# LRU gates of a recurrent block computed by tanh of half their argument

## The chip, the cores and the metric

One core of a Trainium2 chip. The metric is the device time of one execution in microseconds (us); runs of the kernel before and of the changed one are compared. TensorE is called PE, VectorE DVE, ScalarE ACT, GpSimd POOL, SyncE SP.

## What is computed

The program is a small encoder in fp32, of a recurrent block with its feed-forward part and an attention block with its own; the model width is 1024, the sequence 16 meta tokens and 512 others. The change touches the gated linear recurrence (LRU) of the recurrent block, 1536 channels wide:

```python
def rg_lru(x, w_r, b_r, w_i, b_i, lam):
    xb = x.reshape(bsz, length, N_LRU_BLOCKS, LRU_BLOCK)
    r = jax.nn.sigmoid(jnp.einsum('blnc,ncd->blnd', xb, w_r).reshape(bsz, length, width) + b_r)
    i = jax.nn.sigmoid(jnp.einsum('blnc,ncd->blnd', xb, w_i).reshape(bsz, length, width) + b_i)
    log_a = -LRU_C * r.astype(jnp.float32) * jax.nn.softplus(-lam.astype(jnp.float32))
    a = jnp.exp(log_a)
    u = jnp.sqrt(-jnp.expm1(2.0 * log_a)) * (i * x).astype(jnp.float32)
    ...
    _, h = lax.associative_scan(combine, (a, u), axis=1)
    return h.astype(x.dtype)

def recurrent_mixer(x, w_in, conv_w, conv_b, w_r, b_r, w_i, b_i, lam, w_out):
    ...
    rec = causal_dwconv(rec, conv_w, conv_b)
    h = rg_lru(rec, w_r, b_r, w_i, b_i, lam)
    return (jax.nn.gelu(gate) * h) @ w_out
```

There are 16 blocks of 96 channels, and `LRU_C` is 8.

## The kernel before, in words

Channels lie on the 128 partitions and tokens along the free axis, 528 of them, worked on in two halves of 272 and 256. The 1536 recurrent channels are 12 chunks of 128, and three chunks are one group of the LRU. Every number is kept as a high part, rounded to the multiplier's format, and a low part; a product is three matmuls (`project`, L188). Weights come by DMA, 512 KB at a time, into three buffers; ACT casts the high part (L162), and DVE or POOL subtracts for the low part (through the helper `tt`, L118). The helpers `tt` (L118), `stt` (scalar_tensor_tensor, L121) and `act` (L124) record most operations, so in the trace these carry the helper's line.

The recurrent block is cut into steps, each with the number of a chunk or group:

- R, `recurrent_in` (L762): the projection of one chunk, 24 matmuls for each half into a PSUM bank; ACT evacuates the bank with scale and bias, DVE reads it three times more for the convolution's other taps (L775), and `split` (L216) makes high and low parts.
- S, `stack` (L724): eight DMAs on SP's queue gather rows of a group's chunks, so that blocks of 96 channels meet chunks of 128. The LRU step of that group multiplies the gathered rows.
- L, `lru` (L783): for each of three chunks, two gates and two halves, a group of five matmuls and an activation on ACT, twelve in all; then an exponential and a tanh for each chunk, then three square roots, and then on DVE the products and the scan (L823).
- G, `gate_project` (L829): the projection of a chunk of the output gate, evacuated by an ACT copy; E, `gate_gelu` (L853): its gelu; F, `gate_finish` (L858): the product with the LRU's result, and its split.

R and G take their banks in turn from the same four (`gbank(0, 4)`): R6's halves take two, G2's the other two, R7's halves the two of R6 again, each as soon as DVE has read it for the last time. L takes its banks from four others.

Before, ACT goes through three tables in an LRU step: sigmoid for the gates, then exponential and tanh, then square root. The compiler puts an ACT_TABLE_LOAD before each activation that needs another table than the one in place; the gelus of the G and E steps need one as well.

PE's order is written out by hand, as the string below (L39); the other engines' order is found by a scheduler when the kernel is built, from priorities (`tc.high_priority`) and from its own estimates of when work becomes ready. Only the LRU's activations and the gelus are tied to their order in the program (`order="lru"`).

```python
ORDER = "S0 G0 R3 R4 G1 R5 L0 S1 R6 G2 R7 L1 G3 R8 S2 G4 R9 E0 E1 E2 L2 F0 G5 F1 R10 F2 R11 S3 G6 L3 " \
    "E3 E4 E5 G7 F3 G8 F4 F5 G9 E6 E7 E8 F6 F7 F8 G10 E9 F9 G11 E10 F10 E11 F11"
```

Of the kernel before, what the change touches and what calls it, by code (L numbers as in the profile page):

```python
# [8 lines left out]
F32 = mybir.dt.float32  # L9
F32R = mybir.dt.float32r  # L10
AF = mybir.ActivationFunctionType
ALU = mybir.AluOpType
# [5 lines left out]
KD, KR, KF = D // 128, RNN // 128, FF // 128  # L18
# [22 lines left out]
P_ACW, P_ACB, P_BR, P_BI, P_LAM = 0, 48, 60, 72, 84  # L41
# [37 lines left out]
def trunk(ctx: ExitStack, tc: tile.TileContext, d, out):  # L79
    nc = tc.nc  # L80
    const = ctx.enter_context(tc.tile_pool(name="const", bufs=1))
# [13 lines left out]
    prm = const.tile([128, NPRM], F32, name="prm")  # L95
    cst = const.tile([128, 272], F32, name="cst")
    small = const.tile([128, 176], F32, name="small")
# [7 lines left out]
    def col(i):  # L105
        return prm[:, i:i + 1]
# [4 lines left out]
    def kept(x, engine):  # L111

        if line[0]:
            tc.stamp_issue_order_token(x.ins, line[0] + engine)
        return x

    def tt(eng, o, a, b, op):
        return kept(eng.tensor_tensor(o, a, b, op=op), "v" if eng is nc.vector else "p")  # L118

    def stt(o, a, s, b, op0, op1):  # L120
        return kept(nc.vector.scalar_tensor_tensor(o, in0=a, scalar=s, in1=b, op0=op0, op1=op1), "v")  # L121

    def act(o, i, f, order=None, **k):
        x = nc.scalar.activation(o, i, f, **k)  # L124
        if order:
            tc.stamp_issue_order_token(x.ins, order)
            return x
        return kept(x, "a")
# [53 lines left out]
    def mm(ps, w, x, first, last):  # L182
        nc.tensor.matmul(ps, lhsT=w, rhs=x, start=first, stop=last)  # L183
# [42 lines left out]
    def tok(a, n):  # L226
        return slice(PAD + a, PAD + a + n)

    A = slice(PAD, SLOT)
# [16 lines left out]
    def log1p_series(o, e, t1, t2):  # L246

        nc.vector.tensor_scalar(t1, e, 2.0, None, op0=ALU.add)
        nc.vector.reciprocal(t2, t1)
        tt(nc.vector, t1, e, t2, ALU.mult)  # L250
        tt(nc.vector, t2, t1, t1, ALU.mult)
        nc.vector.tensor_scalar(o, t2, 1.0 / 15.0, None, op0=ALU.mult)
        for n in (13, 11, 9, 7, 5, 3):
            stt(o, o, 1.0 / n, t2, ALU.add, ALU.mult)
        stt(o, o, 1.0, t1, ALU.add, ALU.mult)
        nc.vector.tensor_scalar(o, o, 2.0, None, op0=ALU.mult)

    m8, p4 = small[:, 0:12], small[:, 12:24]

    def decay_rates():  # L260
        lam = prm[:, P_LAM:P_LAM + KR]
        w0, w1, w2, w3 = (small[:, 40 + 12 * i:52 + 12 * i] for i in range(4))
        act(w0, lam, AF.Abs)
        act(w0, w0, AF.Exp, scale=-1.0)
        log1p_series(w3, w0, w1, w2)
        nc.vector.tensor_scalar(w1, lam, -1.0, 0.0, op0=ALU.mult, op1=ALU.max)
        tt(nc.vector, w1, w1, w3, ALU.add)
        nc.vector.tensor_scalar(m8, w1, -8.0, None, op0=ALU.mult)
        nc.vector.tensor_scalar(p4, w1, 4.0, None, op0=ALU.mult)
        nc.sync.dma_start(cst, d["cst"])  # L270
        nc.sync.dma_start(fb, d["fb"])

    for k in range(KD):
        w = x32[k // 2][k % 2].f[:, A]
        with tc.high_priority(EARLY):
            nc.sync.dma_start(w, d["x"][k])
        W_rec0.get(3 * k)
        with tc.high_priority(AHEAD):
            split(xs[k], w, A)
        if k == 1:  # L280
            nc.sync.dma_start(prm[:, :P_FC], d["prm"][:, :P_FC])
        if k == KD - 1:
            nc.sync.dma_start(prm[:, P_FC:], d["prm"][:, P_FC:])
            decay_rates()
# [431 lines left out]
    def gbank(first, n):  # L716
        used[first] = used.get(first, -1) + 1
        return fresh_bank(first + used[first] % n)
# [3 lines left out]
    xc, ax, stacks = [], [], {}  # L722
# [60 lines left out]
    def lru(g):  # L783
        gates = []
        for mc in range(3):
            m = 3 * g + mc
            ri = mem.take(F32)
            for gate, bias in ((0, P_BR), (1, P_BI)):
                wh, wl = W_lru.get(2 * g + gate)
                p, e = stacks[g]  # L790
                x, x1 = xc[3 * g + mc], xc[3 * g + 1]
                parts = {0: [(wh, "1", p[0]), (wl, "10", x1[0])], 1: [(wh, "mid", e[0]), (wl, "mid lo", e[0])],
                         2: [(wh, "2", p[1]), (wl, "12", x1[0])]}[mc]
                parts = [(wh, str(11 * mc).zfill(2), x[0]), (wh, str(11 * mc).zfill(2), x[1]), (wl, str(11 * mc).zfill(2), x[0])] + parts
                for t0, n in HALVES:
                    ps = gbank(4, 4)
                    c = tok(t0, n)
                    for i, (w, name, y) in enumerate(parts):
                        o = LRU_AT[name]
                        mm(ps[:, :n], w[:, o:o + 128], y.r[:, c], i == 0, i == len(parts) - 1)  # L800
                    with tc.high_priority(AHEAD):
                        act(ri[gate].f[:, c], ps[:, :n], AF.Sigmoid, bias=col(bias + m), order="lru")
            gates.append(ri)
        W_lru.drop(2 * g + 2)
        scanned.add(g - 1)
        for p in stacks.pop(g):
            p.free()
        for mc in range(3):
            m = 3 * g + mc
            r = gates[mc][0].f[:, A]  # L810
            act(ax[m][0].f[:, A], r, AF.Exp, scale=m8[:, m:m + 1], order="lru")
            act(r, r, AF.Tanh, scale=p4[:, m:m + 1], order="lru")
        for mc in range(3):
            r = gates[mc][0].f[:, A]
            act(r, r, AF.Sqrt, order="lru")
        for mc in range(3):
            m = 3 * g + mc
            r, i = (s.f[:, A] for s in gates[mc].slots)
            a, x = (s.f[:, A] for s in ax[m].slots)
            stt(r, a, 1.0, r, ALU.add, ALU.mult)  # L820
            tt(nc.vector, i, i, x, ALU.mult)
            tt(nc.vector, r, r, i, ALU.mult)
            nc.vector.tensor_tensor_scan(x, a, r, initial=0.0, op0=ALU.mult, op1=ALU.add)  # L823
            gates[mc].free()
            xc[m].free()
# [32 lines left out]
    def gate_finish(m):  # L858
# [9 lines left out]
        ps_in.append(p)  # L868

    steps = {"R": recurrent_in, "S": stack, "L": lru, "G": gate_project, "E": gate_gelu, "F": gate_finish}  # L870
    recurrent_first()
    norm_shifts()
    order = [(step[0], int(step[1:])) for step in ORDER.split()]
# [669 lines left out]
```

## Time and profile before

| | |
|---|---|
| runs | 1404.84, 1407.05, 1408.13 us (median 1407.05) |
| the profiled execution | time 1405.54 us, span 1403.6 us |
| PE busy | 1372.3 us (98% of the span) |
| DVE, ACT, POOL busy | 895.7, 667.2, 170.2 us |
| granted clock of PE, mean | 0.993 of full speed |
| ACT_TABLE_LOADs | 23, 29.5 us together |
| the four LRU steps on PE | between some 57 and 160 us of the span |

The span runs from the first to the last instruction of the profiled execution; its own time is 1.9 us longer. The views cited below are the page's table of busy times; groups of instructions by line (with the idle time of the engine just before them and what ended it); timelines of one engine, where neighbouring instructions of a kind are one row; and windows, with busy times and the granted clock of a stretch. Names in the rows have no buffer numbers: "bank" is PSUM, "g" a working tile, "l" a raw weight buffer, "prm" and "small" columns of parameters. A DMA's row has SPq for SP's queue.

### The profile page before, as it was taken

Reading aid. Unit: us, or ns where it says so; the run is one execution under the profiler, and the core shown is the slowest. Engines: PE = TensorE matmul, PEld = TensorE weight load, DVE = VectorE, ACT = ScalarE, POOL = GpSimd, SP = SyncE. Lnnn points to the kernel's source line nnn. Section 1 sums busy time; section 2 is a strip of 40 time slices with the busy share of each in tenths; the row PEclk is TensorE's granted clock in tenths of the full one; section 3 lists DMA queues with packets and bytes.
Section 4 is the critical chain, followed back from the end, with each engine's and each line's share of the span. In section 5 each row is a group of like instructions: output and inputs, shape, how many; then the busy total and the mean of one; then the engine's idle time right before and its main releaser. Section 6 shows DMA issues by size and latency. Waiting matters only on the chain. (4 is left out here: it accounts for less than half of the span.)

```text
span 1403.6 us, 27111 instructions
## 1 busy us (share of the span) xinstructions
PE 1372.3 (98%) x11118; PEld 1350.7 (96%) x11118; DVE 895.7 (64%) x1717; ACT 667.2 (48%) x1229; POOL 170.2 (12%) x297
## 2 busy tenths in 40 slices
PE   9999899999999999999999999998999999999997
PEld 9998899999999999998999999998899999999997
DVE  7777583886652566637666666778897662556645
ACT  6687751564431344413555556554465441344413
POOL 1000001500000000035311323142200000000021
PEclk9999999999999999999999999999999999999998
DMA  6533353042231422320343425224033231422201
GB/s 214 167 100 97 95 154 102 31 146 96 91 106 49 133 76 76 97 94 16 84 116 85 128 57 149 73 72 139 16 127 125 96 106 61 135 76 91 76 1 61
DMA packets 45163, 133.78 MB, mean 95 GB/s; under 512 B 6064, under 2 KB 9392, under 8 KB 45040
## 3 DMA queue, kind: packets, MB, share of 16 engines
q1 hardware_dynamic: 45040, 132.05, 30.6%
q8 instruction: 88, 1.44, 0.4%
q14 instruction: 35, 0.29, 0.1%
HBM read 115.88 MB, written 2.10 MB: 84 GB/s over the span
## 5 line engine op out<-in xcount | busy, mean ns | idle before, releaser
L183 PE MATMUL bank<-g,g 128*128 128x258 f32 (+7 forms) x10640 | 1327.4, 286 | 17.0 <-DVE g L121 6.9
L183 PEld LDWEIGHTS bank<-g,g 128*128 128x128 f32 (+1 forms) x10640 | 1300.2, 188 | 28.8 <-issue 8.8
L162 ACT CAST g<-l 128x1024 fp32r<-128x1024 f32 (+4 forms) x225 | 226.3, 1010 | 261.0 <-PE bank L183 155.6
L118 DVE TENSOR_TENSOR g<-l,g 128x1024 fp32r<-128x1024 f32 (+3 forms) x209 | 251.9, 1208 | 144.0 <-ACT g L162 107.3
L121 DVE SCALAR_TENSOR_TENSOR g<-bank,prm,g 128x256 f32<-128x256 f32 (+1 forms) x424 | 200.8, 485 | 65.5 <-ACT g L124 60.3
L124 ACT ACTIVATE g<-bank,prm 128x272 f32<-128x272 f32 (+1 forms) x248 | 132.0, 548 | 124.4 <-PE bank L183 123.4
L124 ACT ACTIVATE g<-g 128x528 f32<-128x528 f32 (+9 forms) x237 | 125.6, 545 | 125.5 <-DVE g L118 57.1
L118 DVE TENSOR_TENSOR g<-g,g 128x256 f32<-128x256 f32 (+8 forms) x222 | 125.1, 587 | 43.4 <-ACT g L124 40.7
L124 ACT ACTIVATE g<-bank 128x256 fp32r<-128x256 f32 (+8 forms) x184 | 77.0, 434 | 124.0 <-PE bank L183 116.2
L118 POOL TENSOR_TENSOR g<-g 128x256 f32<-128x256 f32 (+2 forms) x21 | 16.5, 789 | 534.6 <-DVE g L121 516.2
L121 DVE SCALAR_TENSOR_TENSOR g<-g,bank 128x256 f32<-128x256 f32 (+2 forms) x54 | 22.7, 422 | 89.9 <-PE bank L183 89.9
L118 POOL TENSOR_TENSOR g<-g,g 128x272 f32<-128x272 f32 (+2 forms) x72 | 59.1, 835 | 127.4 <-ACT g L124 91.4
L118 POOL TENSOR_TENSOR g<-l,g 128x1024 fp32r<-128x1024 f32 (+2 forms) x16 | 30.7, 1924 | 360.2 <-ACT g L162 333.8
L118 DVE TENSOR_TENSOR g<-bank,g 128x256 fp32r<-128x256 f32 (+6 forms) x100 | 53.9, 541 | 14.0 <-ACT g L124 12.9
L124 ACT ACTIVATE g<-bank,small 128x240 f32<-128x240 f32 (+4 forms) x80 | 38.5, 484 | 40.4 <-DVE small L118 22.8
L1223 POOL TENSOR_SCALAR g<-g,small 128x528 f32<-128x528 f32 (+1 forms) x64 | 36.3, 574 | 143.4 <-DVE small L1222 118.1
L121 DVE SCALAR_TENSOR_TENSOR g<-g,shifts,bank 128x256 f32<-128x256 f32 (+1 forms) x32 | 15.2, 481 | 46.4 <-PE bank L183 46.4
L118 DVE TENSOR_TENSOR g<-g 128x528 f32<-128x528 f32 (+3 forms) x64 | 42.5, 672 | 1.7 <-ACT g L124 0.2
L121 DVE SCALAR_TENSOR_TENSOR g<-g,prm,g 128x256 fp32r<-128x256 f32 (+2 forms) x84 | 42.9, 568 | 1.1 <-ACT g L124 1.1
L124 ACT ACTIVATE g<-g,prm 128x256 fp32r<-128x256 f32 (+3 forms) x64 | 31.0, 509 | 26.4 <-DVE g L121 26.1
L186 PE MATMUL bank<-cst,g 128*128 128x128 f32 (+1 forms) x224 | 33.2, 277 | 2.4 <-DVE mixed L118 1.5
L186 PEld LDWEIGHTS bank<-cst,g 128*128 128x128 f32 (+1 forms) x224 | 23.7, 126 | 8.5 <-issue 2.6
(84 smaller groups left out, 372.5 us busy)
## 6 DMA issues: line engine op xcount, KB each, us to landing
l<-w_fin_d SPq DMA_DIRECT2D x88, 512.0 KB
l<-w_fout_d SPq DMA_DIRECT2D x44, 512.0 KB
g<-g SPq DMA_DIRECT2D x56, 132.0 KB
l<-w_gate_d SPq DMA_DIRECT2D x12, 512.0 KB
l<-w_aout_d SPq DMA_DIRECT2D x12, 512.0 KB
g<-g SPq DMA_DIRECT2D x40, 128.5 KB
l<-w_rec_d SPq DMA_DIRECT2D x9, 512.0 KB
l<-w_k_d SPq DMA_DIRECT2D x8, 512.0 KB
```

The costliest lines, as they stand in the source:

```text
L118: return kept(eng.tensor_tensor(o, a, b, op=op), "v" if eng is nc.vector else "p")
L121: return kept(nc.vector.scalar_tensor_tensor(o, in0=a, scalar=s, in1=b, op0=op0, op1=op1), "v")
L124: x = nc.scalar.activation(o, i, f, **k)
L162: kept(nc.scalar.copy(hi.ap[:, :w], raw.ap[:, :w]), "a")
L183: nc.tensor.matmul(ps, lhsT=w, rhs=x, start=first, stop=last)
L186: nc.tensor.transpose(ps, x, ident[:x.shape[0], :x.shape[0]])
L1223: nc.gpsimd.tensor_scalar(P[ti], P[ti], rc, 0.0, op0=ALU.mult, op1=ALU.add)
```

## The change

The logistic function of z is half of (tanh(z/2) + 1). The gates are now tanh(z/2), by the activation's scale of 0.5 and a bias column `half_bias` that holds half the bias. The "+ 1" and the half move into what uses a gate: the exponential and the tanh of the decay take the factor `m4` (or `p2`), half of what it was, as scale and as bias; the input's product becomes (i + 1) x, and the half goes into the next product. DVE's two tensor_tensor products of a chunk become scalar_tensor_tensor. Gates, exponential and tanh then lie in one table of ACT, and the square root in another.

```diff
--- before.py
+++ after.py
@@ -255,7 +255,8 @@
         stt(o, o, 1.0, t1, ALU.add, ALU.mult)
         nc.vector.tensor_scalar(o, o, 2.0, None, op0=ALU.mult)
 
-    m8, p4 = small[:, 0:12], small[:, 12:24]
+    m4, p2 = small[:, 0:12], small[:, 12:24]
+    half_bias = const.tile([128, 2 * KR], F32, name="half_bias")
 
     def decay_rates():
         lam = prm[:, P_LAM:P_LAM + KR]
@@ -265,8 +266,10 @@
         log1p_series(w3, w0, w1, w2)
         nc.vector.tensor_scalar(w1, lam, -1.0, 0.0, op0=ALU.mult, op1=ALU.max)
         tt(nc.vector, w1, w1, w3, ALU.add)
-        nc.vector.tensor_scalar(m8, w1, -8.0, None, op0=ALU.mult)
-        nc.vector.tensor_scalar(p4, w1, 4.0, None, op0=ALU.mult)
+
+        nc.vector.tensor_scalar(m4, w1, -4.0, None, op0=ALU.mult)
+        nc.vector.tensor_scalar(p2, w1, 2.0, None, op0=ALU.mult)
+        nc.vector.tensor_scalar(half_bias, prm[:, P_BR:P_BR + 2 * KR], 0.5, None, op0=ALU.mult)
         nc.sync.dma_start(cst, d["cst"])
         nc.sync.dma_start(fb, d["fb"])
 
@@ -785,7 +788,7 @@
         for mc in range(3):
             m = 3 * g + mc
             ri = mem.take(F32)
-            for gate, bias in ((0, P_BR), (1, P_BI)):
+            for gate in range(2):
                 wh, wl = W_lru.get(2 * g + gate)
                 p, e = stacks[g]
                 x, x1 = xc[3 * g + mc], xc[3 * g + 1]
@@ -799,7 +802,7 @@
                         o = LRU_AT[name]
                         mm(ps[:, :n], w[:, o:o + 128], y.r[:, c], i == 0, i == len(parts) - 1)
                     with tc.high_priority(AHEAD):
-                        act(ri[gate].f[:, c], ps[:, :n], AF.Sigmoid, bias=col(bias + m), order="lru")
+                        act(ri[gate].f[:, c], ps[:, :n], AF.Tanh, scale=0.5, bias=half_bias[:, KR * gate + m:KR * gate + m + 1], order="lru")
             gates.append(ri)
         W_lru.drop(2 * g + 2)
         scanned.add(g - 1)
@@ -808,8 +811,8 @@
         for mc in range(3):
             m = 3 * g + mc
             r = gates[mc][0].f[:, A]
-            act(ax[m][0].f[:, A], r, AF.Exp, scale=m8[:, m:m + 1], order="lru")
-            act(r, r, AF.Tanh, scale=p4[:, m:m + 1], order="lru")
+            act(ax[m][0].f[:, A], r, AF.Exp, scale=m4[:, m:m + 1], bias=m4[:, m:m + 1], order="lru")
+            act(r, r, AF.Tanh, scale=p2[:, m:m + 1], bias=p2[:, m:m + 1], order="lru")
         for mc in range(3):
             r = gates[mc][0].f[:, A]
             act(r, r, AF.Sqrt, order="lru")
@@ -818,8 +821,8 @@
             r, i = (s.f[:, A] for s in gates[mc].slots)
             a, x = (s.f[:, A] for s in ax[m].slots)
             stt(r, a, 1.0, r, ALU.add, ALU.mult)
-            tt(nc.vector, i, i, x, ALU.mult)
-            tt(nc.vector, r, r, i, ALU.mult)
+            stt(i, i, 1.0, x, ALU.add, ALU.mult)
+            stt(r, r, 0.5, i, ALU.mult, ALU.mult)
             nc.vector.tensor_tensor_scan(x, a, r, initial=0.0, op0=ALU.mult, op1=ALU.add)
             gates[mc].free()
             xc[m].free()
```

In the built program there are 18 ACT_TABLE_LOADs where there were 23: two fewer in L0 and one fewer each in L1, L2 and L3. PE's and POOL's instructions stand in the order they had. On SP's queue a pair of weight loads for R9 and L2 has changed places, and a weight load has passed one of S3's copies. ACT and DVE differ in order between L0 and the last F steps, at three places as follows. Numbers are of tiles and shift by one or two between the two programs.

DVE behind L0, before. g_880 is R6's tile, "bank" a read of its PSUM bank; g_756, g_785 and g_814 are L0's gates; L823 are the scans:

```order
L121 SCALAR_TENSOR_TENSOR g_880<-bank,prm,g_880 128x256 x3
L121 SCALAR_TENSOR_TENSOR g_756<-g_357,g_756 128x528
L118 TENSOR_TENSOR g_756<-g_756 128x528
L121 SCALAR_TENSOR_TENSOR g_785<-g_371,g_785 128x528
L823 SCALAR_TENSOR_TENSOR g_357<-g_357,g_756 128x528
L118 TENSOR_TENSOR g_785<-g_785 128x528
L121 SCALAR_TENSOR_TENSOR g_814<-g_385,g_814 128x528
L823 SCALAR_TENSOR_TENSOR g_371<-g_371,g_785 128x528
L118 TENSOR_TENSOR g_814<-g_814 128x528
L118 TENSOR_TENSOR g_881<-g_880,g_881 128x272
L823 SCALAR_TENSOR_TENSOR g_385<-g_385,g_814 128x528
L118 TENSOR_TENSOR g_881<-g_880,g_881 128x256
```

Now R6's tile is g_882, the gates are g_758, g_787 and g_816, R7's tile is g_1017, and the scans are L826:

```order
L121 SCALAR_TENSOR_TENSOR g_816<-g_387,g_816 128x528
L826 SCALAR_TENSOR_TENSOR g_373<-g_373,g_787 128x528
L121 SCALAR_TENSOR_TENSOR g_816<-g_816 128x528
L118 TENSOR_TENSOR g_883<-g_882,g_883 128x272
L826 SCALAR_TENSOR_TENSOR g_387<-g_387,g_816 128x528
L121 SCALAR_TENSOR_TENSOR g_882<-bank,prm,g_882 128x256
L118 TENSOR_TENSOR g_1083<-l_1081,g_1082 128x1024
L121 SCALAR_TENSOR_TENSOR g_882<-bank,prm,g_882 128x256
L121 SCALAR_TENSOR_TENSOR g_1017<-bank,prm,g_1017 128x272
L121 SCALAR_TENSOR_TENSOR g_882<-bank,prm,g_882 128x256
```

The three reads of R6's second half (128x256) stood ahead of L0's products and scans. They now stand behind the third scan, with a weight's subtraction and a read of R7's first half among them.

ACT in the same stretch, before; the activations with `small` are L0's exponentials and tanhs, the one of g_756 behind the load its first square root:

```order
L124 ACTIVATE g_371<-g_785,small 128x528
L124 ACTIVATE g_880<-bank,prm 128x272
L124 ACTIVATE g_785<-g_785,small 128x528
L124 ACTIVATE g_385<-g_814,small 128x528
L124 ACTIVATE g_880<-bank,prm 128x256
L124 ACTIVATE g_814<-g_814,small 128x528
L124 ACT_TABLE_LOAD
L124 ACTIVATE g_756<-g_756 128x528
```

Now:

```order
L124 ACTIVATE g_387<-g_816,small 128x528
L162 CAST g_1196<-l_1195 128x1024
L124 ACTIVATE g_816<-g_816,small 128x528
L124 ACT_TABLE_LOAD
L124 ACTIVATE g_758<-g_758 128x528
L124 ACTIVATE g_952<-bank 128x272
L124 ACTIVATE g_787<-g_787 128x528
L124 ACTIVATE g_816<-g_816 128x528
L124 ACTIVATE g_883<-g_882 128x272
L124 ACTIVATE g_882<-bank,prm 128x256
```

The evacuation of R6's second half (g_880, now g_882, 128x256) has moved from among the exponentials to behind the third square root, and a weight's cast (L162) stands among the exponentials.

ACT ahead of L3, before; g_1730 is the high part of R11, whose second half is the source of the last two copies of stack S3, and g_1874 is L3's first gate:

```order
L124 ACTIVATE g_1815<-bank 128x256
L162 CAST g_2048<-l_2047 128x1024
L124 ACTIVATE g_1730<-g_1729 128x256
L124 ACT_TABLE_LOAD
L124 ACTIVATE g_1874<-bank,prm 128x272
L124 ACTIVATE g_1874<-bank,prm 128x256
```

Now g_1730 is g_1732 and the gate is g_1876:

```order
L124 ACTIVATE g_1817<-bank 128x256
L162 CAST g_2050<-l_2049 128x1024
L124 ACT_TABLE_LOAD
L124 ACTIVATE g_1876<-bank,half_bias 128x272
L124 ACTIVATE g_1732<-g_1731 128x256
L124 ACTIVATE g_1876<-bank,half_bias 128x256
```

The table load and the first gate's first half stand ahead of that cast; they stood behind it.

## Rows read from the trace of the kernel before

**Rows 1.** The page's first part: busy time of each engine.
```profile
PE 1372.3 (98%) x11118; PEld 1350.7 (96%) x11118; DVE 895.7 (64%) x1717; ACT 667.2 (48%) x1229; POOL 170.2 (12%) x297
```

**Rows 2.** Groups by line, PE, 60 to 160 us: busy, mean ns | idle before, releasers.
```profile
L183 PE MATMUL bank<-g,g 128*128 128x272 f32 (+3 forms) x728 | 93.1, 289 | 7.3 <-DVE g L121 3.2 <-DMA g<-g 2.5 <-ACT g L124 1.5
```

**Rows 3.** Timeline of PE, 60 to 290: start us, us, operation, count [idle before <-releaser].
```profile
59.81 46.38 PE L183 MATMUL bank<-g,g 128*128 128x272 f32 x374
107.61 3.33 PE L183 MATMUL bank<-g,g 128*128 128x276 f32 x24 [1.42 <-DVE g L121]
...
118.19 22.88 PE L183 MATMUL bank<-g,g 128*128 128x272 f32 x184 [1.29 <-ACT g L124]
142.48 6.49 PE L183 MATMUL bank<-g,g 128*128 128x272 f32 x51 [1.40 <-DVE g L121]
...
154.62 88.40 PE L183 MATMUL bank<-g,g 128*128 128x272 f32 x709 [1.87 <-DMA g<-g]
```

**Rows 4.** Groups by line and shape, ACT, whole span.
```profile
L162 ACT CAST g<-l 128x1024 fp32r<-128x1024 f32 x198 | 206.3, 1046 | 247.0 <-PE bank L183 155.3 <-DMA l<-w_fin_d 31.0 <-issue 10.9
...
L124 ACT ACT_TABLE_LOAD x23 | 29.5, 1283 | 1.1 <-PEq L1534 0.7
L124 ACT ACTIVATE g<-g 128x528 f32<-128x528 f32 x44 | 27.0, 638 | 9.3 <-DVE g L121 9.1
...
L124 ACT ACTIVATE g<-g,small 128x528 f32<-128x528 f32 x24 | 17.0, 730 | 0.1
```

**Rows 5.** Timeline of ACT, 0 to 290.
```profile
69.80 0.55 ACT L124 ACTIVATE g<-bank,prm 128x256 f32<-128x256 f32 x1
...
72.29 0.65 ACT L124 ACTIVATE g<-g 128x528 f32<-128x528 f32 x1
...
80.86 0.56 ACT L124 ACTIVATE g<-bank,prm 128x256 f32<-128x256 f32 x1 [2.14 <-PE bank L183]
...
84.95 0.43 ACT L124 ACTIVATE g<-g 128x272 fp32r<-128x272 f32 x1 [0.63 <-DVE g L121]
...
116.36 1.28 ACT L124 ACT_TABLE_LOAD   x1
117.66 1.23 ACT L124 ACTIVATE g<-bank,prm 128x272 f32<-128x272 f32 x3
...
149.85 0.42 ACT L124 ACTIVATE g<-g 128x256 fp32r<-128x256 f32 x1
```

**Rows 6.** Timeline of DVE, 50 to 200.
```profile
62.90 1.16 DVE L118 TENSOR_TENSOR g<-l,g 128x960 fp32r<-128x960 f32 x1 [0.95 <-DMA g<-g]
...
68.67 3.23 DVE L121 SCALAR_TENSOR_TENSOR g<-bank,prm,g 128x272 f32<-128x272 f32 x6 [0.57 <-ACT g L124]
72.97 0.71 DVE L121 SCALAR_TENSOR_TENSOR g<-g,g 128x528 f32<-128x528 f32 x1 [1.06 <-ACT g L124]
73.71 0.71 DVE L118 TENSOR_TENSOR g<-g 128x528 f32<-128x528 f32 x1
...
79.46 1.25 DVE L823 TENSOR_TENSOR_SCAN g<-g,g 128x528 f32<-128x528 f32 x1
...
80.94 1.22 DVE L118 TENSOR_TENSOR g<-l,g 128x1024 fp32r<-128x1024 f32 x1
...
106.99 0.87 DVE L121 SCALAR_TENSOR_TENSOR g<-bank,prm,g 128x272 f32<-128x272 f32 x2
```

**Rows 7.** Timeline of SP's DMA issues, 55 to 130 and 140 to 170.
```profile
60.32 1.19 SPq L735 DMA_DIRECT2D g<-g  x2
...
150.29 1.19 SPq L735 DMA_DIRECT2D g<-g  x2
```

**Rows 8.** Windows: us, busy time by engine, granted clock of PE, DMA share, GB/s.
```profile
106.00:109.00 3.00, 1.58 (x13) 1.42 (x12) 3.00 (x5) 1.90 (x3) 0.00 (x0) 1.00 0.00 0
152.00:154.00 2.00, 0.64 (x3) 0.42 (x3) 0.71 (x1) 2.00 (x5) 0.00 (x0) 1.00 0.60 221
154.00:160.00 6.00, 5.38 (x31) 5.41 (x32) 2.35 (x3) 2.82 (x7) 0.00 (x0) 0.72 0.28 87
```


## The prediction

> **What bounds the kernel now.** I read the busy times first: TensorE (PE) is busy for 1372.3 of 1403.6 us, VectorE (DVE) for 895.7, ScalarE (ACT) for 667.2 [rows 1]. Work taken from ACT or DVE is worth nothing unless PE waits for it. So I read next where PE stands still while the four LRU steps run. From 60 to 160 us its matmuls wait 7.3 us in all: 3.2 for DVE, 2.5 for DMA, 1.5 for ACT [rows 2]. The stops that carry this are 1.42 and 1.40 us behind DVE's reads of a PSUM bank, 1.29 behind an ACT activation, 1.87 behind a DMA [rows 3]. What matters most is what is absent: 374 matmuls run without a stop from 59.81 to 106.19 [rows 3], through all of R7 and L1. PE's and POOL's order is the same before and now; that of ACT and DVE differs between L0 and the last F steps alone, so the sum is made there.
>
> **The change, part by part.** Times are in the profiled execution (span 1403.6, time 1405.54, 1.5 below the median 1407.05).
>
> *Table loads.* 23 become 18. A load is 1.283 us [rows 4]; five are 6.4 us of ACT. Two go in L0 (before the gates, before the exponentials), one each in L1, L2 and L3. One load before the gates stays wherever a square root was the last function, and the one before the square roots always stays. The next activation starts right behind a load: 116.36 + 1.28 = 117.64, and the next starts at 117.66 [rows 5]. The Trainium skill ("ScalarE: Activation LUTs", section "What ACT_TABLE_LOAD costs") gives 1283 ns for the load and about 1380 ns more for a drain; five loads would then be worth 13.3 us of ACT instead of 6.4. The load agrees, the drain doesn't show in these rows.
>
> *Dearer activations.* 24 exponentials and tanhs get a second operand read from a column. An activation of 528 columns takes 638 ns without such an operand and 730 with one [rows 4]. So a second one should add 0.09 each, 0.55 per LRU step (between nothing and 0.1 each). The twelve gate activations of a step had a column as bias before and keep one.
>
> *DVE.* Twenty-four multiplications become scalar_tensor_tensor; on 528 columns both take 0.71 us (72.97 and 73.71 [rows 6]); one operation on 24 columns is added at the start. Nothing, as DVE's other 500 us of idle time cover it; without cover, less than one of these. On SP's queue two pairs of neighbouring transfers have changed places; what they carry is used well over 10 us later, and without that cover it would cost one issue, 0.6 (two take 1.19 [rows 7]).
>
> *The order on ACT and DVE at L0, the largest term.* R6's second half holds a bank that R7's second half takes over. Before, ACT evacuated it among the exponentials at 69.80 [rows 5], and DVE's three reads were the end of the six that start at 68.67 and take 3.23 us [rows 6]; the bank was free at 71.9. R7's second half began without waiting: its evacuation at 80.86 waited for PE [rows 5], and 24 matmuls take 3.33 us at 276 columns [rows 3], so 3.14 at 260: it began at about 77.7. In the new order that evacuation stands behind all three square roots, and the three reads stand behind L0's third scan, with a weight subtraction and a read for R7 between them. When is that? The square roots began at 72.29 [rows 5]. Against that: one load less, -1.28; the other load, -0.4 (it stood before gates that PE paces, so most of it was waiting anyway); R6's evacuation gone, -0.46; a weight cast let in, +0.95 (1.046 by itself [rows 4], its end beside the next); operands, +0.55. Sum -0.64, so 71.65. DVE's burst of three multiplications, products and scans ran from 72.97 to 79.46 + 1.25 = 80.71 [rows 6]; it keeps its content and ends at 80.07. Then one subtraction (1.22, as at 80.94, 1.15 when the next follows at once) and four reads of about 0.4 (two take 0.87 at 106.99 [rows 6]): free at 82.75. R7's second half starts at 82.85 in place of 77.7: **PE is 5.2 later**. Nothing covers it, because PE's order is written out by hand and L1 stands behind R7. The bounds: with two subtractions more ahead of the reads it is 7.5, with the one gone and L0 another load ahead 2.8.
>
> *What later steps give back.* L1's gates come behind R7, so L1's chain on ACT and DVE starts 5.2 late as well. It is shorter: one load, -1.28; operands, +0.55; ACT's waits for DVE among L1's gates (0.63 at 84.95 [rows 5] is the larger) mostly go, as DVE has time to catch up during PE's stop, -0.7. So the reads that end at 106.99 + 0.48 and free R9's bank come 3.8 late. R9's first half stood 1.42 there [rows 3]; PE, 5.2 late, stands for nothing: **-1.4**. L2: the load at 116.36 [rows 5] stood between PE and its gates; it goes, and with it PE's stop of 1.29 [rows 3]: **-1.3** (0 if another cast takes its place). L2's exponentials keep their load and pay 0.55; the stop of 1.40 at 142.48 [rows 3] grows by **0.4**.
>
> *L3's last strips.* L3 starts when the stack's last two strips have been copied. Their source is a cast by ACT at 149.85 [rows 5]; the two copies are issued at 150.29 [rows 7] and PE resumes at 154.62 [rows 3]. In the new order a table load and a gate activation stand ahead of that cast, so the copies are issued 1.8 later. But from 152 to 154 the queues moved 221 GB/s [rows 8], more than two strips of 132 KB: weights were ahead of them. An empty queue was faster: two strips issued at 60.32 [rows 7] were followed by an operation that waited for a transfer until 62.90 [rows 6], 2.6 later at most, against 4.3 here. Coming 1.8 later behind a queue that has drained should give back about 1.2: **+0.6** (0 to 1.8).
>
> *The clock.* Behind the stop of 1.87 before 154.62, which others of the 2.5 us of DMA waits precede closely [rows 2, 3], the granted clock was 0.72 on the mean of 154 to 160 us, between the 2.4 GHz level and the 1.2 one; around the stop of 1.42 it stayed at 1.00 [rows 8]. The lost part is 0.28 of 6 us, 1.7. A stop of 5.2 is nearer to the case at L3, so I charge **1.7** once more (0 to 2.5, half as much again).
>
> **Sum:** 5.2 - 1.4 - 1.3 + 0.4 + 0.6 + 1.7 = **+5.2 us**. From 1405.54 that is 1410.7; the mean of the four executions shown (three runs and the profiled one) is 1406.4, and from it I forecast **1411.6 us**, 4.5 above the median. About 0.2%, 2.8 us, is what a measurement of this kernel can tell from no change.
>
> **The rivals.**
> - *The stop comes, the clock stays full.* For it: 1.42 left the clock alone [rows 8]. 5.2 - 1.7 = +3.5, 1409.9. Chance 0.13.
> - *The strips are as late as their issue, and the last gate step too.* The first takes back the 1.2; for the second I charge half a weight cast (1.046 [rows 4]), since one has moved ahead of the chain behind the last G step. 1.2 + 0.5 more than the sum: 1413.3. For it: nothing shows what else is on the queue by then; against it: the 2.6 us behind 60.32. Chance 0.10.
> - *The other side: R7's bank is free in time.* If the loads saved in L0 bring ACT's and DVE's burst so far forward that the reads end by about 78, the first term and the clock go, and the rest is -1.4 - 1.3 + 0.4 + 0.6 = -1.7: 1404.7, on the edge of what can be told. The sign turns where the first stop and its clock together are 1.7 us in place of 6.9. For it: the square roots, and so the scans, follow straight from ACT's chain, in which two loads fall away. Against it: the scans alone are three times 1.25 [rows 6] and stand ahead of the reads. Chance 0.14.
> - *A load costs more than its record.* If leaving a table took as long again as the load itself, in time that the records put elsewhere, L0's chain would be 2.6 earlier and the stop 2.6, with a third of the clock's 1.7; the sum would be 2.6 - 1.4 - 1.3 + 0.4 + 0.6 + 0.6 = +1.5, 1407.9, no difference. Against it: ACT's idle time ahead of all 23 loads is 1.1 us, and their mean is 1.283 [rows 4]. Chance 0.05. The drain on the Trainium skill's page "ScalarE: Activation LUTs" ("What ACT_TABLE_LOAD costs") would make this case; the rows of this trace speak against it.
>
> **How the numbers follow.** The forecast keeps 0.58: a stop at R7 of 3 to 6 us with a dip of the clock. Range: low end with no dip, the lowest run and a stop that is 1 us shorter, 1404.84 + 3.5 - 1 = 1407; high end, the highest run and the second rival, 1408.13 + 5.2 + 1.2 + 0.5 = 1415. I take 1407 to 1415.5; it leaves out the third rival and the outer parts of the second and of the forecast. Faster by over 0.2% needs 1404.2 or less: a little over half of the third rival, 0.08. Within 0.2% (to 1409.9) are its other part, the fourth rival, and the low parts of the first and of the forecast: 0.21. Slower: 0.71.
>
> **What would show it.** 18 table loads. A new stop of PE, 4 to 6 us, in front of R7's second half near 78 us, ended by a DVE read of the bank; the clock below 1.00 just behind it. The stops before R9 and L2 (1.42, 1.29) gone or under 0.5. PE's resumption at L3 some 3 to 5 us later than 154.62. No gap behind a load. If PE runs through R7 without stopping, the forecast is wrong at its main term; if the stop comes and the total is unchanged, then PE had slack further on that these rows don't show.

## The result and the profile after

The changed kernel took 1414.64 us (median of 4 runs, 1413.48 to 1417.65), the kernel before 1407.02 on the same chip (4 runs): a ratio of 1.0055, interval 1.004 to 1.007. That is 7.6 us slower; 4.5 was forecast against the median shown then. The time lies in the range, near its upper end. The profiled execution took 1414.42, its span 1412.4.

PE's timeline in the changed kernel, as in [rows 3] (start us, us, operation, count, idle before and its releaser):

```profile
49.78 27.60 PE L183 MATMUL bank<-g,g 128*128 128x276 f32 x223
82.61 34.04 PE L183 MATMUL bank<-g,g 128*128 128x260 f32 x252 [5.22 <-DVE g L121]
117.08 28.36 PE L183 MATMUL bank<-g,g 128*128 128x260 f32 x228 [0.44 <-DVE g L121]
147.41 8.68 PE L183 MATMUL bank<-g,g 128*128 128x272 f32 x68 [1.98 <-DVE g L121]
156.69 0.64 PE L183 MATMUL bank<-g,g 128*128 128x272 f32 x3 [0.60 <-ACT g L124]
159.75 88.17 PE L183 MATMUL bank<-g,g 128*128 128x272 f32 x709 [2.43 <-DMA g<-g]
...
263.15 1.18 PE L183 MATMUL bank<-ones,g 128*96 128x1 f32 x12 [1.43 <-DVE g L118]
```

The stop that was absent from [rows 3] is there: 5.22 us in front of R7's second half, ended by a DVE read of its bank. The stops before R9's first half (1.42) and L2 (1.29) are gone, the one before G6 has grown from 1.40 to 1.98, and PE leaves the waits of L3 at 159.75, 5.1 later than before. The last row is a stop that the prediction didn't have, at the first layer norm behind the recurrent block.

The windows behind these stops (columns as in [rows 8]; the eighth figure, ahead of the DMA share, is the granted clock):

```profile
82.00:88.00 6.00, 5.39 (x25) 5.43 (x26) 3.19 (x7) 0.85 (x2) 0.00 (x0) 0.50 0.56 172
158.00:164.00 6.00, 4.25 (x22) 4.28 (x23) 1.93 (x2) 2.81 (x6) 0.00 (x0) 0.72 0.37 110
264.00:274.00 10.00, 10.00 (x61) 10.00 (x61) 6.31 (x15) 3.38 (x7) 4.01 (x5) 0.66 0.17 54
```

Behind the stop at R7, PE works for 5.39 us at 0.50, the 1.2 GHz level: 2.7 us of work lost. At L3 the clock is down as it was before [rows 8]. From 264 to 274 us the clock lost 0.34 of 10 us, 3.4 us of work; before, that stretch ran at 1.00.

So the profiled execution falls behind up to L3 and at the first norm. The same eight matmuls behind the norm, before and then now:

```profile
273.18 1.05 PE L183 MATMUL bank<-cst,small 128*128 128x128 f32 x8
```

```profile
282.28 1.05 PE L183 MATMUL bank<-cst,small 128*128 128x128 f32 x8
```

PE was 5.1 us behind on leaving L3 and is 9.1 behind here; at the end the spans differ by 8.8. The first norm added 4.0, and what comes after it nothing.

ACT's and DVE's timelines behind L0, to be held against [rows 5, 6]:

```profile
69.18 0.83 ACT L124 ACTIVATE g<-g,small 128x528 f32<-128x528 f32 x1
70.04 1.28 ACT L124 ACT_TABLE_LOAD   x1
71.33 0.65 ACT L124 ACTIVATE g<-g 128x528 f32<-128x528 f32 x1
...
73.55 0.55 ACT L124 ACTIVATE g<-bank,prm 128x256 f32<-128x256 f32 x1
```

```profile
78.50 1.25 DVE L826 TENSOR_TENSOR_SCAN g<-g,g 128x528 f32<-128x528 f32 x1
79.67 0.46 DVE L121 SCALAR_TENSOR_TENSOR g<-bank,prm,g 128x256 f32<-128x256 f32 x1
80.05 1.22 DVE L118 TENSOR_TENSOR g<-l,g 128x1024 fp32r<-128x1024 f32 x1
81.18 1.69 DVE L121 SCALAR_TENSOR_TENSOR g<-bank,prm,g 128x256 f32<-128x256 f32 x4
```

The square roots start at 71.33, R6's evacuation follows at 73.55, and its three reads stand behind the third scan with a weight's subtraction (80.05) between them. They were done by 71.9; now the bank is free at about 82.5. This execution runs 0.3 to 0.6 us ahead of the other between 28 and 72 us, so the places agree with the prediction's 71.65, 80.07 and 82.85 to some 0.3.

ACT's groups, as in [rows 4]:

```profile
L124 ACT ACT_TABLE_LOAD x18 | 23.1, 1283 | 1.0 <-PEq L1537 0.7
...
L124 ACT ACTIVATE g<-g,small 128x528 f32<-128x528 f32 x24 | 19.2, 826 | 0.1
```

18 loads of 1.283 us, and 826 ns for an activation with two column operands, 96 more than with one (730) where one cost 92 more than none (638). ACT's work fell by 3.2 us, 667.2 to 664.0, and the kernel became slower by more than twice that.

### The profile page after: what moved, and what is told of

Read it like the earlier page. It is cut to its first block, busy times and chain, and to the rows that moved or that the text cites. A ratio compares the mean times of both kernels' runs of the same rounds, so it can differ in the third digit from the quotient of the medians.

```text
span 1412.4 us, 27107 instructions
## 1 busy us (share of the span) xinstructions
PE 1374.9 (97%) x11118; PEld 1354.3 (96%) x11118; DVE 894.5 (63%) x1718; ACT 664.0 (47%) x1224; POOL 168.1 (12%) x297
## 5 line engine op out<-in xcount | busy, mean ns | idle before, releaser
L162 ACT CAST g<-l 128x1024 fp32r<-128x1024 f32 (+4 forms) x225 | 226.4, 1010 | 254.7 <-PE bank L183 150.5
L124 ACT ACTIVATE g<-bank,prm 128x272 f32<-128x272 f32 (+1 forms) x200 | 111.3, 564 | 123.7 <-PE bank L183 123.3
L118 DVE TENSOR_TENSOR g<-g,g 128x256 f32<-128x256 f32 (+8 forms) x210 | 117.3, 582 | 38.7 <-ACT g L124 32.3
L121 DVE SCALAR_TENSOR_TENSOR g<-g,g 128x528 f32<-128x528 f32 (+4 forms) x46 | 29.1, 641 | 24.1 <-ACT g L124 23.8
L118 DVE TENSOR_TENSOR g<-g 128x528 f32<-128x528 f32 (+4 forms) x52 | 34.4, 666 | 1.7 <-ACT g L124 0.2
```

Of the source, the lines that this page charges most:

```text
L162: kept(nc.scalar.copy(hi.ap[:, :w], raw.ap[:, :w]), "a")
```

## The experiments

The theory: the scheduler's new order at R6 makes PE stand, and the clock falls behind that; the functions themselves cost nothing. The rival: the new functions cost the time.

**1. The changed kernel with R6's reads put back.** One priority; nothing else moves on ACT and DVE beyond what follows from it.

```diff
-            act(x.f[:, c], ps[:, 4:n + 4], AF.Identity, scale=col(P_ACW + 36 + m), bias=col(P_ACB + m))
-            for j in (2, 1, 0):
-                stt(x.f[:, c], ps[:, j + 1:j + 1 + n], ...
+            with tc.high_priority(EARLY) if m == 6 and t0 else nullcontext():
+                act(x.f[:, c], ps[:, 4:n + 4], AF.Identity, scale=col(P_ACW + 36 + m), bias=col(P_ACB + m))
+                for j in (2, 1, 0):
+                    stt(x.f[:, c], ps[:, j + 1:j + 1 + n], ...
```

> The changed kernel, with the evacuation and the three reads of R6's second half put back ahead of L0's square roots and scans; nothing else moves. Theory A (the order at R6 is the cause): no stop of PE in front of R7's second half (5.22 us in the changed kernel), the granted clock at 1.00 from 76 to 90 us where it fell to 0.50, and R9's stop back at under 1.42. That takes 5.2 and 2.7 us away and gives up to 1 back: 1406 to 1408 if the stop of 1.43 at the first layer norm (263 us) stays with its dip of the clock, 1403 to 1405 if that one was a coincidence of DVE and POOL. Rival B (the new functions themselves cost it: dearer activations, scalar_tensor_tensor products): the time stays within 1.5 of 1414.6.

Measured 1407.2 (10 runs, 1405.5 to 1409.75), ratio to the kernel before 1.001, interval 0.9998 to 1.0021. Its PE timeline, and its window behind the place of the stop:

```profile
49.81 59.28 PE L183 MATMUL bank<-g,g 128*128 128x276 f32 x475
109.52 28.35 PE L183 MATMUL bank<-g,g 128*128 128x260 f32 x228 [0.44 <-DVE g L121]
139.85 6.44 PE L183 MATMUL bank<-g,g 128*128 128x272 f32 x51 [1.97 <-DVE g L121]
...
152.20 88.17 PE L183 MATMUL bank<-g,g 128*128 128x272 f32 x709 [2.41 <-DMA g<-g]
```

```profile
84.00:86.00 2.00, 2.00 (x17) 1.90 (x17) 1.97 (x6) 1.52 (x5) 0.00 (x0) 1.00 0.80 215
```

No stop at R7, none before R9's first half, the clock full. The loss is gone with the order: against the kernel before, 1.0055 has become 1.001, some 6.3 us of the 7.6, with the new functions still in place. The functions are not the cause. One thing missed: PE leaves L3 at 152.20, 2.4 earlier than before, and the stop at the first norm was 0.28 without a dip, so 1403 to 1405 was expected. It came out at 1407.2. What is gained ahead of L3 is not in the total.

**2. Matmuls in the stop.** 18 matmuls of constant ones into an unused bank, whose result nobody reads, ahead of R7's second half; the trace counts two for each, 36.

```diff
+                if m == 7 and t0:
+                    keep_warm(fresh_bank(7), 18)
                 project(ps[:, :n + 4], W_rec, (m - 3) * KD, xs, slice(t0, t0 + n + 4))
```

> The changed kernel with 18 extra matmuls of the constant ones into an unused bank, between R7's first and second half, so that PE works in most of the stop; the order of everything else is as it was. Theory A (the clock falls because PE stood still): the stop in front of R7's second half shrinks to under 1 us, that half starts at the same time (82.6 us), the granted clock stays at 1.00 from 82 to 88 us, PE resumes at L3 some 2.7 us earlier than 159.75, and the time is 1412 or less. Rival B (the clock fell for another reason, such as the DMA burst that starts at 82 us): the clock still falls and the time stays at 1414.6, or more if the extra matmuls hold up R7.

```profile
77.84 4.18 PE L203 MATMUL bank<-ones 128*128 128x128 f32 x36
83.23 31.66 PE L183 MATMUL bank<-g,g 128*128 128x260 f32 x252 [1.21 <-DVE g L121]
```

```profile
82.00:88.00 6.00, 4.79 (x40) 4.80 (x40) 4.78 (x10) 2.44 (x4) 0.00 (x0) 1.00 0.55 169
```

R7's second half starts where it did (83.23; this execution was 0.6 later by then) with 1.21 us of the stop left, not under 1, and behind it the clock is 1.00 while the DMA queues move 169 GB/s, as many as in the changed kernel (172). So the clock fell because PE stood, not because of the transfers. The 252 matmuls that took 34.04 us take 31.66, 2.4 less, and PE left L3 at 157.99, 2.4 earlier if the 0.6 is taken off. The total doesn't show it: 1413.96 is not the 1412 or less expected, and the ratio to the kernel before on the same chip, 1.0062 (1.0045 to 1.0079), is no lower than the changed kernel's 1.0055.

**3. The order alone, with the sigmoids.** The kernel before, with the evacuation of R6's second half tied behind L0's square roots.

```diff
-            act(x.f[:, c], ps[:, 4:n + 4], AF.Identity, scale=col(P_ACW + 36 + m), bias=col(P_ACB + m))
+            act(x.f[:, c], ps[:, 4:n + 4], AF.Identity, scale=col(P_ACW + 36 + m), bias=col(P_ACB + m), order="lru" if m == 6 and t0 else None)
```

> The kernel before, with its sigmoids and its 23 table loads, and one thing changed: the evacuation of R6's second half is tied behind L0's square roots, and DVE's reads follow it behind L0's scans. Theory A: a stop of PE of 5 to 6.5 us in front of R7's second half (L0's chain keeps its two further loads, so the bank is free up to 1 us later than in the changed kernel), a dip of the clock worth 2.7 behind it, and R9's stop of 1.42 mostly still there: 1413 to 1416 against 1407.0. Rival B: 1407, within 1.5.

```profile
85.01 30.73 PE L183 MATMUL bank<-g,g 128*128 128x260 f32 x228 [6.11 <-DVE g L121]
116.65 3.32 PE L183 MATMUL bank<-g,g 128*128 128x276 f32 x24 [0.90 <-DVE g L121]
```

```profile
84.00:92.00 8.00, 6.99 (x36) 7.02 (x37) 4.37 (x10) 2.24 (x4) 0.00 (x0) 0.57 0.42 129
```

1414.79 (ratio 1.0067, 1.005 to 1.0085): the old arithmetic with the new order is as slow as the changed kernel. The stop is 6.11, 0.9 longer, as L0 keeps its two further loads, and R9's stop shrinks from 1.42 to 0.90 only, as L1 keeps its load. Both ends are as the theory has them.

**4. L3's cast ahead of its load.** The changed kernel with the cast of R11's second half tied into the order of the LRU's activations.

```diff
-                split(p, x.f[:, c], c)
+                split(p, x.f[:, c], c, order="lru" if m == 11 and t0 else None)
```

> The changed kernel, with the cast that feeds the last two copies of stack S3 put back ahead of L3's table load and first gate. Theory A (the copies are held up by their issue): they are issued 1.5 to 1.8 us earlier, the DMA stop of 2.43 us before L3 shrinks by 0.6 to 1.8, and the time is 0.6 to 1.8 below 1414.6. Rival B (the copies are held up by the weights on the queue ahead of them): the copies land when they did, and the stop and the time stay.

```profile
158.46 0.65 PE L183 MATMUL bank<-g,g 128*128 128x272 f32 x3 [1.09 <-ACT g L124]
159.43 86.80 PE L183 MATMUL bank<-g,g 128*128 128x272 f32 x709 [0.32 <-DMA g<-g]
```

The issue of the last two copies, in the changed kernel and then in this one:

```profile
156.96 1.19 SPq L738 DMA_DIRECT2D g<-g  x2
```

```profile
156.63 1.19 SPq L738 DMA_DIRECT2D g<-g  x2
```

The wait for DMA falls by 2.1 us, more than expected, and the one for ACT grows by 0.5, so the stops before L3 are 1.6 shorter. In both kernels PE resumes 2.8 us after the copies are issued (159.75 and 159.43): their issue holds them up, as the theory had it. The total doesn't tell: 1413.58 is within the 0.6 to 1.8 expected below 1414.6, but the ratio to the kernel before, 1.0054 (1.0037 to 1.007), is the changed kernel's.

**5 and 6. Both kernels again, word for word.**

> The changed kernel, word for word, for a second profile. In its first profile PE stood 1.43 us at the first layer norm (263 us) and the clock dipped behind that, 4.2 us together; in the four kernels since then the same stop was 0.28 to 0.58 without a dip. Theory A (there DVE and POOL collide differently from one execution to the next): the stop is 0.3 to 0.6 this time, with no dip at 264 to 274 us, while the stop of 5.2 in front of R7's second half and its dip (1.5 to 2.9) are there again; time 1412 to 1415. Rival B (the change causes that stop): 1.4 us and the dip again.

> The kernel before, word for word, for a second profile and for what a comparison of a kernel with itself gives. Ratio 1.000 with an interval of 0.1 to 0.2% to either side. The granted clock dipped at 154, 974, 1014 and 1394 us in the first profile, 5.8 us lost together. Theory A (the dips behind the layer norms and the attention come by chance): the dip at 154 is there again, the later ones are at other places, and the sum lies between 4 and 8. Rival B: the same four.

The changed kernel: 1415.12 (6 runs), ratio 1.0056, 1.004 to 1.0072. Its second profile:

```profile
83.67 34.05 PE L183 MATMUL bank<-g,g 128*128 128x260 f32 x252 [5.23 <-DVE g L121]
...
264.73 1.18 PE L183 MATMUL bank<-ones,g 128*96 128x1 f32 x12 [1.42 <-DVE g L118]
```

The stop at the norm is no accident of one execution: 1.42 again, with 3.4 lost to the clock behind it again. Theory A fell. The time lies just above its 1412 to 1415. The kernel before against itself: ratio 1.0001, 0.9991 to 1.0012, so a comparison tells some 0.1%. The dip at 154 us came again; of those at 974, 1014 and 1394 none did, and one at 656 had come. Over the whole span, 5.8 us of PE's work were lost to the lower clock in the first profile of that kernel (added up over windows of 2 us) and 3.2 in the second, less than the 4 to 8 expected.

**7. Both orders put right.** The edits of 1 and 4 in the changed kernel.

> The changed kernel with both orders put back: R6's second half ahead of L0's square roots, and the cast for S3's last copies ahead of L3's table load. Theory A: no stop at R7; the stops before L3 fall from 3.2 (first of these runs) to some 1.4, as in the run with the cast alone; PE leaves L3 some 4 us earlier than before (about 150.5 against 154.62), 1 to 2 more if the dip of the clock behind L3 goes too. Time 1403 to 1405.5 against 1406.5. Rival B (what is gained at L3 is lost again at the next wait): 1406 to 1407.

1403.64 (9 runs, 1401.68 to 1406.36), ratio 0.9973, 0.9962 to 0.9984: faster than the kernel before.

```profile
109.62 28.34 PE L183 MATMUL bank<-g,g 128*128 128x260 f32 x228 [0.44 <-DVE g L121]
139.93 6.46 PE L183 MATMUL bank<-g,g 128*128 128x272 f32 x51 [1.98 <-DVE g L121]
146.69 2.29 PE L183 MATMUL bank<-g,g 128*128 128x272 f32 x17 [0.30 <-DMA g<-g]
149.54 0.65 PE L183 MATMUL bank<-g,g 128*128 128x272 f32 x3 [0.57 <-ACT g L124]
151.56 86.86 PE L183 MATMUL bank<-g,g 128*128 128x272 f32 x709 [1.37 <-DMA g<-g]
```

```profile
152.00:158.00 6.00, 6.00 (x51) 6.00 (x50) 3.34 (x4) 5.03 (x10) 0.00 (x0) 1.00 0.41 103
```

PE leaves L3 at 151.56, not at 150.5 as expected (the stops there are 2.24, not 1.4), and the clock behind L3 is full, where it had dipped in the kernel before.

**8. And R10's reads ahead of L2's scans.** Beside the edits of 7:

```diff
-            with tc.high_priority(EARLY) if m == 6 and t0 else nullcontext():
+            with tc.high_priority(EARLY if m == 6 else 800) if (m == 6 and t0) or m == 10 else nullcontext():
```

> As the run before, and DVE's reads of R10 also ahead of L2's scans, so that G6 finds its bank free. Theory A: the stop of 1.97 us before G6 falls under 0.7 and the time is 1 to 1.5 below that of the run before. Rival B (the DMA of S3's copies, which then ends last): G6 starts earlier, PE stands as much longer before L3, and the time stays within 0.5 of the run before.

```profile
144.65 2.44 PE L183 MATMUL bank<-g,g 128*128 128x272 f32 x18 [0.34 <-DVE g L118]
149.17 0.65 PE L183 MATMUL bank<-g,g 128*128 128x272 f32 x3 [2.08 <-ACT g L124]
151.94 88.22 PE L183 MATMUL bank<-g,g 128*128 128x272 f32 x709 [2.12 <-DMA g<-g]
...
255.38 1.18 PE L183 MATMUL bank<-ones,g 128*96 128x1 f32 x12 [1.42 <-DVE g L118]
```

The stop before G6 is gone and comes back at L3: 2.08 + 2.12 in place of 0.57 + 1.37, and PE leaves L3 at 151.94, 0.4 later than in 7. The rival was right there. The time was worse than that, 1408.02 (ratio 1.0008, 0.9996 to 1.0019), and this profile has the 1.42 at the first norm.

**9 to 11. A small POOL operation at the first norm.** POOL adds up squares there while DVE centres the rows. In the kernel before POOL's first addition took 0.79 us; in the changed one:

```profile
250.86 2.20 POOL L118 TENSOR_TENSOR g<-g,g 128x272 f32<-128x272 f32 x1 [10.38 <-ACT g L124]
```

DVE's side of the same moment, in the kernel before and then in the changed one:

```profile
244.31 3.35 DVE L118 TENSOR_TENSOR g<-g,g 128x272 f32<-128x272 f32 x6
247.59 1.93 DVE L121 SCALAR_TENSOR_TENSOR g<-g,g 128x272 f32<-128x272 f32 x2
```

```profile
249.53 2.20 DVE L118 TENSOR_TENSOR g<-g,g 128x272 f32<-128x272 f32 x6
251.64 0.79 DVE L121 SCALAR_TENSOR_TENSOR g<-g,g 128x272 f32<-128x272 f32 x2
```

Where POOL waits, DVE's eight operations take 2.9 us; where POOL goes ahead, they take 5.2. The edit, in the changed kernel (9), in that of 8 (10) and in that of 7 (11):

```diff
                 act(x, r, AF.Square)
+                if m == 1 and h == 0 and self.base == P_LN:
+                    tt(e, nudge, x[:, :16], x[:, :16], ALU.add)
                 tt(e, q, q, x, ALU.add)
```

> The changed kernel and one more POOL operation, an addition of 16 columns ahead of POOL's first addition at the first layer norm, which starts that addition a tenth of a us or so later. In both profiles of the changed kernel that addition took 2.20 us (0.79 in the kernel before), DVE ran undisturbed beside it, and PE stood 1.42 us behind it, with 3.4 lost to the clock. Theory A (DVE and POOL hold each other up there, and which of the two is held up hangs on a small difference of time): the addition takes under 1.2 us, the stop at the first layer norm is under 0.7 without a dip of the clock at 262 to 276 us, and the time falls by 3 to 4.5, to 1410.5 to 1412. Rival B (the change itself makes this norm slow): the stop of 1.4 and the dip stay, and the time is 1415 as before.

In 9:

```profile
251.44 0.23 POOL L118 TENSOR_TENSOR nudge<-g 128x16 f32<-128x16 f32 x1 [10.37 <-ACT g L124]
251.63 0.96 POOL L118 TENSOR_TENSOR g<-g,g 128x272 f32<-128x272 f32 x1
```

```profile
262.93 1.18 PE L183 MATMUL bank<-ones,g 128*96 128x1 f32 x12 [0.63 <-DVE g L118]
```

```profile
264.00:274.00 10.00, 9.46 (x78) 9.19 (x78) 8.75 (x21) 5.40 (x11) 4.63 (x5) 1.00 0.17 55
1002.00:1010.00 8.00, 8.00 (x42) 7.82 (x41) 4.48 (x15) 1.57 (x5) 0.00 (x0) 0.57 0.00 0
```

The addition is short again, the stop 0.63, the clock full: an operation of 0.23 us ahead of the addition decides it, as theory A had it. But the time is 1414.65 (ratio 1.0061, 1.0046 to 1.0076). In this execution the clock fell between 1002 and 1010 us instead, 3.4 us, where the changed kernel had run at 1.00. The price that theory A put on the norm, 3 to 4.5 us, does not show, and the mean granted clock of these six executions, 0.988, is no higher than the changed kernel's 0.990.

> The kernel with the orders of R6, L3 and R10 put right, and the same small POOL operation. Its profile without it had the addition's long form, the stop of 1.42 and a dip of 3.4. Theory A: stop under 0.7, no dip at 252 to 268 us, and a time 3 to 4.5 below 1408.0: 1403.5 to 1405. Rival B: 1408 as before.

> The kernel with the orders of R6 and L3 put right (1403.6), and the same small POOL operation, which it doesn't need: in its profile DVE had been held up, and PE did not stop. Theory A (the operation matters only through which of the two engines is held up): either nothing changes (1403 to 1404.5) or the other form comes, with the stop of 1.4, the dip and 1407 to 1408. Rival B (the operation costs or gains by itself): a change of 0.5 to 2 us without a change of form.

In 10 the form changed as well (stop 0.64), and the time went from 1408.02 to 1406.96, not by 3 to 4.5 (ratio 0.9999, 0.9988 to 1.001). In 11 the form stayed as it was (stop 0.36), and the time was 1405.85 (ratio 0.999, 0.9979 to 1.0), 2.2 above that of 7, outside what theory A gave and just beyond rival B's 2. That the operation costs this by itself is not shown: the interval overlaps that of 7, and the version of 7, taken again, gave 0.9985 (run 12), in between.

**12. The version of 7 again.**

> The changed kernel with the orders of R6 and L3 put back, word for word as in the run that gave 1403.64, since it is the one version that beat the kernel before. Theory A (the gain is real): a ratio to the kernel before of 0.996 to 0.9985 again, PE out of L3 at 151.0 to 152.0 us, no stop at R7, no dip of the clock behind L3. Rival B (a lucky set of runs; what is gained ahead of 240 us is lost at the later norms): 0.999 to 1.001.

1404.05 (12 runs, 1400.97 to 1407.49), ratio 0.9985, 0.9973 to 0.9998: faster than the kernel before a second time, by less, at the upper end of theory A's range. PE left L3 at 153.10, not at 151 to 152, in an execution that was 1.4 later than that of 7 from R9 on (111.02 against 109.62); no stop at R7, no dip behind L3.

## Why the prediction was right, and where its sizes were off

- **The order at R6 and R7** was the largest term, and it was right: 5.2 forecast, 5.22 and 5.23 measured. Runs 1 and 3 show it as the cause from both sides: put back, the loss is gone; put into the old arithmetic, it is there.
- **The clock** was the term with the wrong size. It was charged with one dip of 1.7 and a bound of 2.5; behind R7 alone 2.7 us of work were lost (run 2 shows that the stop is what draws it). The row that the 1.7 was taken from, the dip behind L3, belongs to stops of 2.7 us in all; in run 4 the dip behind the same stop of 5.2 cost 1.5, in run 3 behind 6.1 it cost 2.9.
- **What later steps give back**: R9's stop went (-1.4), L2's went (-1.3), G6's grew by 0.58 (+0.4 forecast), and the waits before L3 grew from 2.73 to 3.03, +0.3 (+0.6 forecast). Rows for each of them agree, and PE left L3 5.1 us later, where the sum said 5.2. That is closer than its terms: the clock was 1.0 too low, and the execution had been up to 0.6 ahead before the stop.
- **What the sum left out**: it ends at L3 and was taken for the whole. In the profiled execution the first layer norm adds 4.0 us, a stop of 1.43 and a dip of 3.4 that no term stands for. That the time came near the upper end of the range, whose top was built on other terms (the highest run and the second rival), is in part luck.
- **The clock over all executions** points the same way. Each execution's time multiplied by what its mean granted clock lacks to 1 gives the clock's share: on average 9.3 us in the kernel before (89 executions), 14.7 in the changed one (10), so 5.5 more, where 1.7 was charged; 3 to 4 us of each fall at the end of the span, where PE hardly works. Not all of it is time: among executions of one kernel, a microsecond more of it goes with half a microsecond of time (182 executions, each against the mean of its kernel and session). At that rate the 5.5 are worth some 2.7 of the 7.6 us, an estimate; the stops, 3.4 more up to L3 and 1.4 at the norm by the rows, are of the size of the rest.
- **Where run 1's gain gets lost** is settled in part. PE is still 2.2 us ahead at 631 us of the old time; a dip at 654 us costs most of that (3.4 of work), another at 956 us loses 1.7, and PE is behind by some 1040 us. Over its ten executions the clock's share is 10.6 us against 8.1 in the kernel before on the same chip: 2.4 more, at the rate above 1.2 of the 2.4 gained; the rest stays open. Whether an earlier start draws more dips, or these were chance, the runs don't tell; run 9 shows that one such loss removed can be followed by another of the same size.
- **The rivals.** That R7's bank would be free in time did not come about. That the strips are as late as their issue: run 4 shows that they are held up by it, 1.6 us, but against the kernel before only 0.3 of it was a loss, since PE now resumed 2.8 us after the issue in place of 4.3 [rows 3, 7]. A load that costs more than its record: after the change, too, the next activation starts at once (70.04 + 1.28, then 71.33), L0's chain became shorter by what its loads' durations say, and the idle time ahead of all 18 loads is 1.0 us. The drain that the Trainium skill gives ("ScalarE: Activation LUTs", section "What ACT_TABLE_LOAD costs"), about 1380 ns for each switch, is not seen in either kernel.

## What to carry to other kernels

Where a scheduler orders engines, a change that shortens work can reorder it; look at what the new order puts in front of the reads that free a buffer for the bottleneck. A saving off the bottleneck's path (here 6.4 us of table loads) was worth nothing until two orders were put back by hand, and then some 2 to 4 us in 1406 (runs 7 and 12). A stop of TensorE is to be charged with the clock behind it as well: at R7 half as much again. And a kernel whose executions differ by several microseconds from dips at changing places hides a gain of two: the profile shows such a gain where it arises, the total only over many runs.

## What was not expected of the hardware

The collision of DVE and POOL at the first norm has two forms that differ by 2.3 us on DVE (some 2.9 against 5.2 for the same eight operations). Three programs were profiled twice, and each had the same form both times; it changed with edits 100 us ahead of it. When POOL's long form came (2.20), PE's stop behind it was 1.42 to 1.43 and the clock fell, 3.4 us; in the other form (0.79 to 0.96) the stop was 0 to 0.64 and it didn't. The Trainium skill ("SBUF — State Buffer", section "SBUF: two separate sides") says that the two engines share a pair of ports, held as a lock for a whole instruction by whichever starts first, where DVE's operation has two inputs in SBUF and POOL's reads SBUF, as here. The durations fit that (2.20 or 3.35 us for six of DVE's operations, 2.20 or 0.79 for POOL's one, each long where the other is short). But in the long form POOL's addition, begun at 250.86 in the midst of DVE's eight operations, ended at 253.06, 0.6 behind the last of them (252.43): it waited through several, not one. Which of the two is held up is what the small operation of runs 9 and 10 moved.

The granted clock fell behind stops of 1.42 at the norm and 1.85 to 2.4 at L3, and stayed up behind 1.42 at R9 [rows 3, 8] and 1.37 at L3 (run 7). Behind the stop of 1.95 to 1.98 before G6 it fell in run 4 (0.57 from 148 to 152 us) and in none of runs 1, 2, 5, 7, 9, 11 and 12. The length of one stop alone doesn't decide it.
